# Sliding and forgetting attention: logits from stacked high and low parts, and value products issued together

## The chip, the cores and the metric

The kernel runs as one launch on one core of a Trainium2 chip. The metric is device time in microseconds (us). The median of three runs of the kernel before is 2165.17 us (2159.99 to 2167.82).

## The reference, cut to what matters

The network has two layers. Each mixes 512 tokens of width 1024 by four branches (sliding-window attention, a recurrence called rwkv, forgetting attention, and attention over selected keys), gates and merges them, and runs a feed-forward part: a dense one in the first layer, eight experts in the second. The change touches the two attention branches below, and one step that the third attention branch (`dsa`) shares with them.

```python
def swa_branch(q, k, v, sinks):        # 8 heads, 2 key heads, width 64, window of 128 + chunk of 64
    ...
    logits = jnp.einsum('bcqhgd,bckhd->bchgqk', q, kb).astype(jnp.float32) * ATTN_SCALE
    logits = jnp.where(valid[None, :, None, None, None, :], logits, -jnp.inf)
    m = jnp.maximum(jnp.max(logits, axis=-1, keepdims=True), sink)
    e = jnp.exp(logits - m)
    p = e / (jnp.sum(e, axis=-1, keepdims=True) + jnp.exp(sink - m))
    o = jnp.einsum('bchgqk,bckhd->bcqhgd', p.astype(v.dtype), vb)

def fox_branch(q, k, v, f_logit, f_bias):   # 4 heads of width 64
    log_f = jax.nn.log_sigmoid(f_logit.astype(jnp.float32) + f_bias)
    c = jnp.cumsum(log_f, axis=1).transpose(0, 2, 1)
    for blk in range(S // FOX_BLOCK):       # blocks of 128 queries, keys up to the block's end
        logits = jnp.einsum('bqhd,bkhd->bhqk', q[:, lo:hi], k[:, :hi]).astype(jnp.float32) * ATTN_SCALE
        logits = logits + c[:, :, lo:hi, None] - c[:, :, None, :hi]
        logits = jnp.where(causal, logits, -jnp.inf)
        p = jax.nn.softmax(logits, axis=-1)
        outs.append(jnp.einsum('bhqk,bkhd->bqhd', p.astype(v.dtype), v[:, :hi]))
```

## The kernel before

All of a layer's tokens are kept transposed, split into a high part (`xh`, rounded to the type fp32r) and a low part (`xl`, what is left). A projection (`proj_b`) loads a block of 128 columns of `w_in`, splits it into `whi` (ScalarE, L98) and `wlo` (VectorE, L99) and issues 8 times three matmuls of 512 columns (`mm3`, L111 to L113). Gates, branch outputs and the feed-forward part are made of the same three matmuls.

A mixer runs projections for rwkv, then the rwkv recurrence (a long chain of small matmuls; it inverts 64x64 blocks on VectorE, `invert16`, with stores and loads through memory that GpSimd issues, L737 to L759, and PE takes the result up at L849), the values of all branches (`v_proj`), forgetting attention (`fox`), sliding attention (`swa`), the index of the selected keys (`index`), attention over them (`dsa`), and the merge. The program is written in this order; a scheduler of the framework sets the order of each engine's instructions when the kernel is built, by priority and by when it expects operands. The recurrence has the highest priority, so that PE's row of instructions mixes it with attention and with projections and gates. Engines then run their rows strictly in that order.

In `fox` and `swa`, queries and keys of two heads share a tile of 128 rows, 64 rows to a head, in full fp32 (`qk`, `dup`). The logits of one head and one block of 128 queries are one matmul that contracts 64 rows (L584 in `fox`, L540 in `swa`), with 128 to 512 columns, added in PSUM to a mask (L583, L536) and in `fox` to the sums of the forget gates (L582, with the selector `sel`). `dsa` and `index` already use the other form: `qk_split` puts a head's high part in 64 rows and its low part in the other 64, `dup_split` puts the high part of a key twice above each other and likewise the low part, and `dot` (L425, L426) adds two fp32r matmuls that contract 128 rows. `attend` (L462 to L490) is the softmax: maximum on VectorE, exponential on ScalarE, scaling on VectorE, transposes on PE (L487) and a copy. `quad` runs a block for the four heads of two tiles: with up to 256 keys two heads to a call of `attend`, above that one. Its value products (L512) contract 128 keys and give 64 rows each, the even head in PSUM rows 0 to 63, the odd head in rows 64 to 127. PSUM holds one buffer each of `ps_s` (logits), `ps_t` (transposes) and `ps_o` (outputs).

Of the kernel before, what the change touches and what calls it, by code (L numbers as in the profile page):

```python
# [9 lines left out]
F32 = mybir.dt.float32  # L10
# [8 lines left out]
P = 128  # L19
# [17 lines left out]
TAGS = dict(rw=26, qk=10, o=12, pt=7, v=4, x=8, lc=4)  # L37
# [19 lines left out]
class Net:  # L57
# [292 lines left out]
    def mixer(self, layer):  # L350
# [20 lines left out]
    def qk(self, layer, c0):  # L371

        out = []
        for j in range(2):
            ps = self.proj_b(layer, (c0 + j * P, P))
            t = self.bt("qk")
            with self.tc.high_priority():
                self.nc.scalar.copy(t, ps)
            out.append(t)
        return out  # L380

    def qk_split(self, layer, c0, tag):
# [4 lines left out]
        for j in range(2):  # L387
# [10 lines left out]
    def dup(self, ps):  # L398

        nc = self.nc  # L400
        out = []
        for par, me, ot in HALVES:
            t = self.bt("qk")
            nc.scalar.copy(t[0:64], ps[me])
            nc.vector.tensor_copy(t[64:128], ps[me])
            out.append(t)
        return out

    def dup_split(self, ps):

        nc = self.nc
        out = []
        for par, me, ot in HALVES:
            h, l = self.bt("qk", F32R), self.bt("qk", F32R)
            nc.scalar.copy(h[me], ps[me])
            nc.vector.tensor_sub(l[me], ps[me], h[me].bitcast(F32))
            nc.scalar.copy(h[ot], h[me])
            nc.vector.tensor_copy(l[ot], l[me])
            out.append((h, l))
        return out  # L420

    def dot(self, ps, q, k, b, nk, start):

        q = q[:, b * P:(b + 1) * P]
        self.nc.tensor.matmul(ps, q, k[0][:, :nk], start=start, stop=False)  # L425
        self.nc.tensor.matmul(ps, q, k[1][:, :nk], start=False, stop=True)  # L426
# [65 lines left out]

    def quad(self, b, nk, logits, kblocks, vcol, o, nsink=None):

# [4 lines left out]
        for g0 in range(0, 2, nhu):  # L499
# [28 lines left out]
    def swa(self, layer, kv, q, k):  # L528
# [19 lines left out]
    def fox(self, layer, q, k):  # L548
        nc = self.nc

# [19 lines left out]
        cx, ct = self.bt("pt", F32R), self.bt("pt", F32R)  # L570
# [15 lines left out]
        for g in range(2):  # L586
            self.tap(f"o_fox{g}", o[g][0].bitcast(F32))
# [1266 lines left out]
```

## Time and profile before

| | |
|---|---|
| median of three runs | 2165.17 us |
| the profiled execution's own time | 2165.19 us |
| its span in the trace | 2163.5 us |
| PE busy | 2090.9 us, 97% |
| DVE busy | 1343.8 us, 62% |
| ACT busy | 902.2 us, 42% |
| POOL busy | 151.9 us, 7% |

PE is TensorE's matmuls, PEld its weight loads, DVE VectorE, ACT ScalarE, POOL GpSimd. Matmuls overlap in the trace: an entry's duration runs to its last result, while the next one starts earlier. What a matmul costs the engine is therefore read from start to start. An entry `64*128 64x512` names the rows that are contracted and the columns of the array in use (64*128), and then the rows and columns of the operand that streams. A group in a timeline gives the number of records at its end.

### The profile page before, as it was taken

What the parts mean: (1) busy time and instruction counts of PE and PEld (TensorE: products, weight loads), DVE (VectorE), ACT (ScalarE), POOL (GpSimd) and SP (SyncE); (2) the same over time, 40 slices, a digit from 0 to 9 for tenths busy, and PEclk for the clock granted to TensorE, in tenths of its full rate; (3) what the DMA queues carried; (4) which work ended last, traced back from release to release, by engine and by line L of the source; (5) the groups of instructions that cost most, each with busy time, mean ns of one, the idle gap of its engine ahead of it and who ended that gap; (6) DMA issues with size and microseconds to landing.
All of it is one profiled execution on the core that took longest, in us unless ns stands there. A gap on an engine that the chain in (4) does not pass through costs nothing. (4 is left out here: it accounts for less than half of the span.)

```text
span 2163.5 us, 31132 instructions
## 1 busy us (share of the span) xinstructions
PE 2090.9 (97%) x11252; PEld 1598.0 (74%) x11252; DVE 1343.8 (62%) x2688; ACT 902.2 (42%) x1551; POOL 151.9 (7%) x211
## 2 busy tenths in 40 slices
PE   8999999999999999999999999999998999999994
PEld 7766667778888888888776667778886667677663
DVE  5755678744463333236664678844577877788778
ACT  3444532332332222213444443332326666677663
POOL 1020110000000000000001110000000000000034
PEclk9999999999999999999999999999999999999997
DMA  5220112243343333334221112223258888898872
GB/s 168 76 62 26 46 52 76 78 124 96 97 151 98 98 97 106 116 96 121 75 55 33 46 53 69 69 78 98 92 188 309 298 291 326 302 325 314 291 274 86
DMA packets 275535, 295.07 MB, mean 136 GB/s; under 512 B 23908, under 2 KB 203976, under 8 KB 275368
## 3 DMA queue, kind: packets, MB, share of 16 engines
q1 hardware_dynamic: 268296, 274.42, 39.1%
q0 software_dynamic: 7072, 18.49, 2.7%
q8 instruction: 97, 1.59, 0.3%
q14 instruction: 70, 0.57, 0.1%
HBM read 277.26 MB, written 15.60 MB: 135 GB/s over the span
## 5 line engine op out<-in xcount | busy, mean ns | idle before, releaser
L99 DVE TENSOR_TENSOR wlo<-wraw,whi 128x1024 fp32r<-128x1024 f32 (+1 forms) x218 | 265.7, 1219 | 388.9 <-ACT whi L98 378.5
L113 PE MATMUL ps_mm<-xh,wlo 128*128 128x512 f32 (+1 forms) x1288 | 496.5, 386 | 3.1 <-DVE rs L259 3.1
L98 ACT CAST whi<-wraw 128x1024 fp32r<-128x1024 f32 (+1 forms) x218 | 228.1, 1046 | 650.5 <-PE ps_mm L112 403.1
L111 PE MATMUL ps_mm<-xh,whi 128*128 128x512 f32 (+1 forms) x1288 | 496.4, 386 | 0.8 <-ACT whi L98 0.4
L112 PE MATMUL ps_mm<-xl,whi 128*128 128x512 f32 (+1 forms) x1288 | 494.6, 384 | 0.5 <-DVE xl L233 0.5
L113 PEld LDWEIGHTS ps_mm<-xh,wlo 128*128 128x128 f32 x1288 | 243.3, 189 | 53.1 <-issue 7.7
L111 PEld LDWEIGHTS ps_mm<-xh,whi 128*128 128x128 f32 x1288 | 243.5, 189 | 52.8 <-issue 8.8
L112 PEld LDWEIGHTS ps_mm<-xl,whi 128*128 128x128 f32 x1288 | 243.6, 189 | 48.8 <-issue 5.5
L1153 DVE TENSOR_TENSOR wlo<-mwraw,whi 128x1024 fp32r<-128x1024 f32 (+1 forms) x98 | 124.2, 1281 | 18.0 <-ACT whi L1152 15.6
L1152 ACT CAST whi<-mwraw 128x1024 fp32r<-128x1024 f32 (+1 forms) x98 | 95.9, 1005 | 15.5 <-PE ps_t L1503 9.7
L490 ACT COPY bt_pt<-ps_t 128x512 f32<-128x512 f32 (+2 forms) x80 | 41.8, 522 | 129.5 <-PE ps_t L487 128.8
L462 DVE TENSOR_REDUCE mx<-ps_s 128x2 f32<-128x512 f32 (+3 forms) x80 | 48.7, 609 | 53.5 <-PE ps_s L584 21.4
L1153 DVE TENSOR_TENSOR mwlo<-mwraw,mwhi 128x1024 fp32r<-128x1024 f32 (+1 forms) x62 | 71.9, 1175 | 6.5 <-ACT mwhi L1152 6.0
L471 ACT ACTIVATE bt_pt<-ps_s,mx 128x256 f32<-128x256 f32 (+3 forms) x128 | 62.2, 489 | 18.3 <-DVE mx L465 7.4
L260 POOL TENSOR_TENSOR rs<-rs,mhalf 128x1 f32<-128x1 f32 x16 | 13.8, 860 | 699.0 <-DVE rs L259 699.0
L1152 ACT CAST mwhi<-mwraw 128x1024 fp32r<-128x1024 f32 (+1 forms) x62 | 61.0, 998 | 3.0 <-DMA mwraw<-in_exp_w_dram 1.8
L512 PE MATMUL ps_o<-bt_pt,bt_v 128*64 128x128 f32 (+1 forms) x408 | 60.7, 322 | 0.4 <-ACT bt_pt L490 0.4
L1114 DVE TENSOR_TENSOR bt_pt<-bt_pt,ps_mm 128x512 f32<-128x512 f32 x22 | 15.1, 688 | 70.7 <-PE ps_mm L113 63.3
L612 DVE MAX8 m<-bt_pt 128x8 f32<-128x256 f32 (+2 forms) x96 | 53.5, 558 | 2.1
L1153 DVE TENSOR_TENSOR wlo<-ring,whi 128x1024 fp32r<-128x1024 f32 (+1 forms) x45 | 51.4, 1159 | 2.5 <-ACT whi L1152 1.5
L613 DVE MATCH_REPLACE8 bt_pt<-m,bt_pt 128x256 f32<-128x256 f32 (+2 forms) x96 | 52.1, 543 | 0.0
L112 PE MATMUL ps_mm<-bt_o,whi 128*128 128x512 f32 x128 | 51.5, 402 | 0.0
(716 smaller groups left out, 4133.8 us busy)
## 6 DMA issues: line engine op xcount, KB each, us to landing
mwraw<-in_exp_w_dram SPq DMA_DIRECT2D x124, 512.0 KB, 6.5
wraw<-in_w_in_dram SPq DMA_DIRECT2D x106, 512.0 KB, 3.5
wraw<-in_ffn_w_dram SPq DMA_DIRECT2D x66, 512.0 KB, 3.7
ring<-in_exp_w_dram SPq DMA_DIRECT2D x60, 512.0 KB, 6.4
wraw<-in_exp_w_dram SPq DMA_DIRECT2D x32, 512.0 KB, 7.0
mwraw<-in_exp_w_dram SPq DMA_DIRECT2D x36, 384.0 KB, 5.6
wraw<-in_w_branch_dram SPq DMA_DIRECT2D x20, 512.0 KB, 3.5
wraw<-in_w_out_dram SPq DMA_DIRECT2D x16, 512.0 KB, 3.6
```

Of the source, the lines that this page charges most:

```text
L98: nc.scalar.copy(h, src)
L99: (low or nc.vector).tensor_sub(l, src, h.bitcast(F32))
L111: mm(ps, wh, xh, start=start, stop=False)
L112: mm(ps, wh, xl, start=False, stop=False)
L113: mm(ps, wl, xh, start=False, stop=stop)
L462: nc.vector.tensor_reduce(mx[:, 0:nh], s3, op=OP.max, axis=AX.X)
L471: nc.scalar.activation(p3[:, h], s3[:, h], AF.Exp, bias=nm[:, h:h + 1], scale=0.125, accum_out=mx[:, 4 + h:5 + h])
L512: nc.tensor.matmul(ot[64 * par:64 * par + 64, (g0 + h) * P:(g0 + h + w) * P], self.v[kblocks[kb]][:, c:c + 64], pts[par][:, i * P:(i + w) ...
L612: nc.vector.max(m8, sc[:, :nk])
L613: nc.vector.match_replace(sc[:, :nk], m8, sc[:, :nk], REPL)
L1152: self.chain("hi", lambda: nc.scalar.copy(hi[:, :n], src))
L1153: self.chain("lo", lambda: nc.vector.tensor_sub(lo[:, :n], src, hi[:, :n].bitcast(F32)))
```

## The change

Both attention branches take the form that `dsa` had. `fox` runs once per group of two heads instead of once for four: `forget` makes the forget sums first, and each group then has one tile of queries by `qk_split` and one of keys by `dup_split`. `swa` gets its keys by `dup_split` and its queries by `qk_split`. `dot` gains an offset of the first key. `dup_split` makes the high and the low part of both heads first, at high priority, and the copies to the other 64 rows after. In `quad` and `fox` the value products go through `sums`: it starts with the odd head, whose softmax is made last, alternates the heads, and ties all later products of the block behind the first (`issue_after`), for `dsa` too. Eight kilobytes more per partition are held by tiles of the tag `qk` (14 instead of 10 tiles of 512 fp32), and the scratch in which GpSimd writes its DMA descriptors is set to 8192 bytes per partition (before, the framework's default of 16384).

```diff
-TAGS = dict(rw=26, qk=10, o=12, pt=7, v=4, x=8, lc=4)
+TAGS = dict(rw=26, qk=14, o=12, pt=7, v=4, x=8, lc=4)
...
-        fq, fk = self.qk(layer, FOX0), self.qk(layer, FOX0 + 256)
-        self.fox(layer, fq, fk)
-        sk = self.dup(self.proj_b(layer, (SWA0 + 512, P)))
+        self.forget()
+        for g in range(2):
+            q, = self.qk_split(layer, FOX0 + g * P, "qk", 1)
+            k = self.dup_split(self.proj_b(layer, (FOX0 + 256 + g * P, P)))
+            self.fox(g, q, k)
+        sk = self.dup_split(self.proj_b(layer, (SWA0 + 512, P)))
         for kv in range(2):
-            q = self.qk(layer, SWA0 + 256 * kv)
-            self.swa(layer, kv, q, sk[kv])
+            q = self.qk_split(layer, SWA0 + 256 * kv, "qk")
+            self.swa(kv, q, sk[kv])
         iq = self.qk_split(layer, DSA0 + 384, "qk")
         k, ik = self.dup_split(self.proj_b(layer, (DSA0 + 256, 64), (DSA0 + 640, 64)))
...
-    def qk(self, layer, c0):
-
+    def qk_split(self, layer, c0, tag, n=2):
+
+
+        nc = self.nc
         out = []
-        for j in range(2):
-            ps = self.proj_b(layer, (c0 + j * P, P))
-            t = self.bt("qk")
-            with self.tc.high_priority():
-                self.nc.scalar.copy(t, ps)
-            out.append(t)
-        return out
-
-    def qk_split(self, layer, c0, tag):
-
-
-        nc = self.nc
-        out = []
-        for j in range(2):
+        for j in range(n):
             ps = self.proj_b(layer, (c0 + j * P, P))
             t = [self.bt(tag, F32R) for _ in range(2)]
             with self.tc.high_priority():
...
     def dup_split(self, ps):
 
         nc = self.nc
-        out = []
-        for par, me, ot in HALVES:
-            h, l = self.bt("qk", F32R), self.bt("qk", F32R)
-            nc.scalar.copy(h[me], ps[me])
-            nc.vector.tensor_sub(l[me], ps[me], h[me].bitcast(F32))
+        out = [(self.bt("qk", F32R), self.bt("qk", F32R)) for _ in HALVES]
+        with self.tc.high_priority():
+            for (par, me, ot), (h, l) in zip(HALVES, out):
+                nc.scalar.copy(h[me], ps[me])
+                nc.vector.tensor_sub(l[me], ps[me], h[me].bitcast(F32))
+        for (par, me, ot), (h, l) in zip(HALVES, out):
             nc.scalar.copy(h[ot], h[me])
             nc.vector.tensor_copy(l[ot], l[me])
-            out.append((h, l))
         return out
 
-    def dot(self, ps, q, k, b, nk, start):
-
+    def dot(self, ps, q, k, b, nk, start, k0=0, skip=False):
+
+        mm = self.nc.tensor.matmul
         q = q[:, b * P:(b + 1) * P]
-        self.nc.tensor.matmul(ps, q, k[0][:, :nk], start=start, stop=False)
-        self.nc.tensor.matmul(ps, q, k[1][:, :nk], start=False, stop=True)
+        mm(ps, q, k[0][:, k0:k0 + nk], start=start, stop=skip, skip_group_check=skip)
+        mm(ps, q, k[1][:, k0:k0 + nk], start=False, stop=True, skip_group_check=skip)
...
+    def sums(self, args):
+
+        mm = self.nc.tensor.matmul
+        first = None
+        for ps, v, p, start, stop in args:
+            with ExitStack() as st:
+                if first is not None:
+                    st.enter_context(self.tc.issue_after(first.ins))
+                m = mm(ps, v, p, start=start, stop=stop)
+            first = first or m
+
...
-            w = nhu if vcol(0, 0) == vcol(1, 0) else 1
-            for h in range(0, nhu, w):
-                for kb in range(nkb):
-                    for par in range(2):
-                        c = vcol(g0 + h, par)
-                        i = kb * nhu + h
-                        nc.tensor.matmul(ot[64 * par:64 * par + 64, (g0 + h) * P:(g0 + h + w) * P],
-                                         self.v[kblocks[kb]][:, c:c + 64], pts[par][:, i * P:(i + w) * P],
-                                         start=kb == 0, stop=kb == nkb - 1)
+            self.sums([(ot[64 * par:64 * par + 64, g0 * P:(g0 + nhu) * P], self.v[kblocks[kb]][:, vcol:vcol + 64],
+                        pts[par][:, kb * nhu * P:(kb + 1) * nhu * P], kb == 0, kb == nkb - 1)
+                       for kb in range(nkb) for par in (1, 0)])
...
-                r = slice(64 * par, 64 * par + 64)
                 for g in gs:
-                    nc.tensor.matmul(s3[:, g], q[g][r, b * P:(b + 1) * P], k[r, kbl[0] * P:(b + 1) * P], start=False,
-                                     stop=True, skip_group_check=True)
-
-            self.quad(b, nk, logits, kbl, lambda g, par: VC_SWA + kv * 64, o,
+                    self.dot(s3[:, g], q[g][par], k, b, nk, False, kbl[0] * P, True)
...
+    def forget(self):
+
+        nc = self.nc
         z = self.bp.tile([P, 3, TB, 4], F32, name="fz", tag="fz")
...
-        cx, ct = self.bt("pt", F32R), self.bt("pt", F32R)
-        nc.scalar.activation(cx, cps, AF.Copy, scale=-8.0)
+        self.cx, ct = self.bt("pt", F32R), self.bt("pt", F32R)
+        nc.scalar.activation(self.cx, cps, AF.Copy, scale=-8.0)
...
+    def fox(self, g, q, k):
+
+        nc = self.nc
+        o = self.new_o(("fox", g))
         for b in range(TB):
             nk = P * (b + 1)
-
-            def logits(gs, par, s, s3, b=b, nk=nk):
-                r = slice(64 * par, 64 * par + 64)
-                for i, g in enumerate(gs):
-                    nc.tensor.matmul(s3[:, i], self.sel[:, 2 * g + par:2 * g + par + 1].to_broadcast([P, P]), cx[:, :nk], start=True, stop=False)
+            nh = 2 if nk <= 256 else 1
+            pts = []
+            for p0 in range(0, 2, nh):
+                s = self.ps("s")
+                s3 = s[:, :nh * nk].rearrange("p (h k) -> p h k", h=nh)
+                for i in range(nh):
+                    h = 2 * g + p0 + i
+                    nc.tensor.matmul(s3[:, i], self.sel[:, h:h + 1].to_broadcast([P, P]), self.cx[:, :nk], start=True,
+                                     stop=False)
                     nc.tensor.matmul(s3[:, i, b * P:], self.identb, self.m_causal, start=False, stop=False)
-                    nc.tensor.matmul(s3[:, i], q[g][r, b * P:(b + 1) * P], k[g][r, :nk], start=False, stop=True)
-            self.quad(b, nk, logits, list(range(b + 1)), lambda g, par: VC_FOX + (2 * g + par) * 64, o)
-        for g in range(2):
-            self.tap(f"o_fox{g}", o[g][0].bitcast(F32))
+                    self.dot(s3[:, i], q[p0 + i], k[p0 + i], b, nk, False)
+                pt = self.attend(s3, nh, nk)
+                pts += [[pt[:, (kb * nh + i) * P:(kb * nh + i + 1) * P] for kb in range(b + 1)] for i in range(nh)]
+            ot = self.ps("o")
+            c = VC_FOX + 2 * g * 64
+            self.sums([(ot[64 * par:64 * par + 64, 0:P], self.v[kb][:, c + 64 * par:c + 64 * par + 64], pts[par][kb],
+                        kb == 0, kb == b) for kb in range(b + 1) for par in (1, 0)])
+            self.put_o(o, slice(b * P, (b + 1) * P), ot[:, 0:P])
...
-    nc = bacc.Bacc("TRN2", target_bir_lowering=False, num_devices=1)
+    nc = bacc.Bacc("TRN2", target_bir_lowering=False, num_devices=1, dynamic_dma_scratch_size=8192)
```

The next piece is PE's row in the first layer at the end of `fox`, before. `L584` are logits, `L512` value products, `L849` the recurrence, `L111` to `L113` projections; the number after x counts equal instructions in a row.

```order
L849 MATMUL ps_r<-bt_rw 64x64
L512 MATMUL ps_o<-bt_pt,bt_v 64x128 x7
L582 MATMUL ps_s<-bt_pt,sel 128x512
L583 LDWEIGHTS identb
L583 MATMUL ps_s<-m_causal,identb 128x128
L584 MATMUL ps_s<-bt_qk 128x512
L849 MATMUL ps_r<-bt_rw 64x64 x15
L487 MATMUL ps_t<-ident,bt_pt 128x128 x4
L111 MATMUL ps_mm<-xh,whi 128x512
L112 MATMUL ps_mm<-xl,whi 128x512
L849 MATMUL ps_r<-bt_rw 64x64 x16
L512 MATMUL ps_o<-bt_pt,bt_v 64x128
```

The same engine, changed kernel, at the end of a group of `fox`: `L407` and `L408` are the two matmuls of `dot`, `L483` value products, `L469` transposes.

```order
L575 MATMUL ps_s<-bt_pt,sel 128x128
L577 LDWEIGHTS identb
L577 MATMUL ps_s<-m_causal,identb 128x128
L407 MATMUL ps_s<-bt_qk 128x128
L408 MATMUL ps_s<-bt_qk 128x128
L469 MATMUL ps_t<-ident,bt_pt 128x128 x4
L575 MATMUL ps_s<-bt_pt,sel 128x128
L577 LDWEIGHTS identb
L577 MATMUL ps_s<-m_causal,identb 128x128
L407 MATMUL ps_s<-bt_qk 128x128
L408 MATMUL ps_s<-bt_qk 128x128
L483 MATMUL ps_o<-bt_pt,bt_v 64x128 x8
```

The single matmul over 64 rows has become two over 128 rows. Of a block's eight value products one stood alone (the last row before is the first of the next block) and seven together; now all eight stand together.

Next, PE's row in `swa`, first layer, before: `L540` are logits of two heads, `L512` value products.

```order
L512 MATMUL ps_o<-bt_pt,bt_v 64x256
L113 MATMUL ps_mm<-xh,wlo 128x512
L111 MATMUL ps_mm<-xh,whi 128x512
L536 LDWEIGHTS identb
L536 MATMUL ps_s<-m_swa,identb 128x512
L540 MATMUL ps_s<-bt_qk 128x256 x2
L487 MATMUL ps_t<-ident,bt_pt 128x128 x4
L112 MATMUL ps_mm<-xl,whi 128x512
L113 MATMUL ps_mm<-xh,wlo 128x512
L111 MATMUL ps_mm<-xh,whi 128x512
L112 MATMUL ps_mm<-xl,whi 128x512
L512 MATMUL ps_o<-bt_pt,bt_v 64x256 x3
```

And in the changed kernel, with the recurrence's `L819` near by:

```order
L524 LDWEIGHTS identb
L524 MATMUL ps_s<-m_swa,identb 128x512
L407 MATMUL ps_s<-bt_qk 128x256
L408 MATMUL ps_s<-bt_qk 128x256
L407 MATMUL ps_s<-bt_qk 128x256
L408 MATMUL ps_s<-bt_qk 128x256
L112 MATMUL ps_mm<-xl,whi 128x512
L819 MATMUL ps_r<-bt_rw 128x128 x4
L113 MATMUL ps_mm<-xh,wlo 128x512
L469 MATMUL ps_t<-ident,bt_pt 128x128 x4
```

The two logits of 64 rows after the mask have become four matmuls of `dot`. Over PE's whole row the shape of the array (64 or 128 rows contracted by 32, 64 or 128 columns) changes from one instruction to the next 725 times before and 530 times now, counted over the whole program, branches that are not taken included. The value products of all three branches, 136 of 128 columns and 68 of 256, stand before in 85 unbroken rows: 20 of one, 2 of three, 8 of five and 10 of seven with 128 columns, and 31 of one, 5 of two and 9 of three with 256. Now they stand in 46: 4 of two, 6 of four, 8 of six and 7 of eight, and 2 of one, 5 of two and 14 of four. VectorE has 44 instructions more and ScalarE 28 more; GpSimd and the DMA queue of SyncE have as many as before.

## Rows read from the trace of the kernel before

**Rows 1.** Page, parts 1 and 2: PE busy; granted clock by slice.
```profile
PE 2090.9 (97%) x11252; PEld 1598.0 (74%) x11252; DVE 1343.8 (62%) x2688; ACT 902.2 (42%) x1551; POOL 151.9 (7%) x211
...
PEclk9999999999999999999999999999999999999997
```

**Rows 2.** Windows: us; busy us of PE, PEld, DVE, ACT, POOL; clock, DMA.
```profile
100.00:200.00 100.00, 99.82 (x739) 68.68 (x737) 55.01 (x165) 41.72 (x118) 12.55 (x22) 1.00 0.18 48
200.00:300.00 100.00, 99.31 (x679) 67.24 (x679) 67.70 (x240) 45.32 (x139) 14.61 (x24) 1.00 0.18 48
300.00:415.00 115.00, 112.61 (x638) 86.02 (x635) 97.10 (x241) 37.98 (x77) 2.95 (x2) 0.99 0.26 73
```

**Rows 3.** Waits of PE, 100 to 300 us: total us, times, longest.
```profile
PE ps_r L886 <- ACT xak L880: 0.7, 1, 0.7
```

**Rows 4.** Timeline of PE from 168 us: start us, us, instruction, records.
```profile
168.03 0.40 PE L582 MATMUL ps_s<-bt_pt,sel 128*128 128x512 f32 x1
168.28 0.23 PE L583 MATMUL ps_s<-m_causal,identb 128*128 128x128 bf16 x1
168.44 1.12 PE L584 MATMUL ps_s<-bt_qk 64*128 64x512 f32 x2
169.49 0.50 PE L113 MATMUL ps_mm<-xh,wlo 128*128 128x512 f32 x1
169.82 0.60 PE L487 MATMUL ps_t<-ident,bt_pt 128*128 128x128 f32 x4
...
170.49 0.40 PE L112 MATMUL ps_mm<-xl,whi 128*128 128x512 f32 x1
170.73 0.40 PE L113 MATMUL ps_mm<-xh,wlo 128*128 128x512 f32 x1
171.06 0.33 PE L849 MATMUL ps_r<-bt_rw 64*64 64x64 f32 x2
171.31 1.09 PE L512 MATMUL ps_o<-bt_pt,bt_v 128*64 128x128 f32 x14
172.33 0.50 PE L582 MATMUL ps_s<-bt_pt,sel 128*128 128x512 f32 x1
```

**Rows 5.** Timeline of PE at 252 us: one pair of sliding-window logits.
```profile
252.05 1.13 PE L540 MATMUL ps_s<-bt_qk 64*128 64x256 f32 x4
253.10 0.50 PE L111 MATMUL ps_mm<-xh,whi 128*128 128x512 f32 x1
```

**Rows 6.** Timeline of PE at 288 us: one dot of the index, then projection.
```profile
288.42 0.28 PE L425 MATMUL ps_s<-bt_qk 128*128 128x256 f32 x1
288.53 0.28 PE L426 MATMUL ps_s<-bt_qk 128*128 128x256 f32 x1
288.66 0.40 PE L113 MATMUL ps_mm<-xh,wlo 128*128 128x512 f32 x1
```

**Rows 7.** Timeline of PE at 130 us: one value product of 128 columns alone.
```profile
130.49 0.43 PE L512 MATMUL ps_o<-bt_pt,bt_v 128*64 128x128 f32 x2
130.85 0.50 PE L112 MATMUL ps_mm<-xl,whi 128*128 128x512 f32 x1
```

**Rows 8.** Timeline of PE at 184 us: one value product of 256 columns alone.
```profile
183.90 0.65 PE L512 MATMUL ps_o<-bt_pt,bt_v 128*64 128x256 f32 x2
184.48 0.33 PE L876 MATMUL ps_r<-bt_rw 64*64 64x64 f32 x4
```

**Rows 9.** Groups by line, DVE, 100 to 300 us: busy us, mean ns.
```profile
L394 DVE TENSOR_TENSOR bt_qk<-ps_mm,bt_qk 64x512 fp32r<-64x512 f32 x4 | 2.8, 689 | 0.1
...
L418 DVE CAST bt_qk<-bt_qk 64x512 fp32r<-64x512 f32 x2 | 0.8, 422 | 0.1
```

**Rows 10.** Groups by line, ACT, 100 to 300 us.
```profile
L392 ACT CAST bt_qk<-ps_mm 64x512 fp32r<-64x512 f32 x4 | 2.3, 583 | 0.0
```

**Rows 11.** Timeline of POOL from 152 us: start us, us, records.
```profile
152.52 3.98 POOL L756 DMA_DIRECT2D inv<-bt_rw  x7 [19.45 <-DVE bt_pt L481]
```

**Rows 12.** Line L759, its DMAs: issue to landing.
```profile
DMA to landing us min/median/max: 2.7/2.9/3.5
```

More of the change, by code (lines that the diff above doesn't have):

```diff
@@ L396, in qk_split @@
         return out
-    def dup(self, ps):
-        nc = self.nc
-        out = []
-        for par, me, ot in HALVES:
[L403 to L407, printed above, removed]
     def dup_split(self, ps):
         nc = self.nc
-        out = []
-        for par, me, ot in HALVES:
-            h, l = self.bt("qk", F32R), self.bt("qk", F32R)
-            nc.scalar.copy(h[me], ps[me])
-            nc.vector.tensor_sub(l[me], ps[me], h[me].bitcast(F32))
+        out = [(self.bt("qk", F32R), self.bt("qk", F32R)) for _ in HALVES]
[4 more added lines that the diff above has]
+        for (par, me, ot), (h, l) in zip(HALVES, out):
             nc.scalar.copy(h[ot], h[me])
             nc.vector.tensor_copy(l[ot], l[me])
-            out.append((h, l))
         return out
-    def dot(self, ps, q, k, b, nk, start):
+    def dot(self, ps, q, k, b, nk, start, k0=0, skip=False):
+        mm = self.nc.tensor.matmul
         q = q[:, b * P:(b + 1) * P]
-        self.nc.tensor.matmul(ps, q, k[0][:, :nk], start=start, stop=False)
-        self.nc.tensor.matmul(ps, q, k[1][:, :nk], start=False, stop=True)
+        mm(ps, q, k[0][:, k0:k0 + nk], start=start, stop=skip, skip_group_check=skip)
+        mm(ps, q, k[1][:, k0:k0 + nk], start=False, stop=True, skip_group_check=skip)
     def v_proj(self, layer):
@@ L526, in put_o, with swa @@
         self.nc.vector.tensor_sub(lo[:, ts], ps, hi[:, ts].bitcast(F32))
-    def swa(self, layer, kv, q, k):
+    def swa(self, kv, q, k):
         nc = self.nc
@@ L537, in logits @@
                                  self.m_swa[:, None, 256 - nk:].to_broadcast([P, 2, nk]), start=True, stop=True)
-                r = slice(64 * par, 64 * par + 64)
                 for g in gs:
-                    nc.tensor.matmul(s3[:, g], q[g][r, b * P:(b + 1) * P], k[r, kbl[0] * P:(b + 1) * P], start=False,
-                                     stop=True, skip_group_check=True)
-            self.quad(b, nk, logits, kbl, lambda g, par: VC_SWA + kv * 64, o,
+                    self.dot(s3[:, g], q[g][par], k, b, nk, False, kbl[0] * P, True)
+            self.quad(b, nk, logits, kbl, VC_SWA + kv * 64, o,
                       lambda g0, par, n: self.nsink[:, 4 * kv + par:4 * kv + 4:2])
@@ L546, in swa @@
             self.tap(f"o_swa{2 * kv + g}", o[g][0].bitcast(F32))
-    def fox(self, layer, q, k):
+    def forget(self):
         nc = self.nc
@@ L569, in fox @@
                                  stop=True, skip_group_check=True)
-        cx, ct = self.bt("pt", F32R), self.bt("pt", F32R)
-        nc.scalar.activation(cx, cps, AF.Copy, scale=-8.0)
+        self.cx, ct = self.bt("pt", F32R), self.bt("pt", F32R)
+        nc.scalar.activation(self.cx, cps, AF.Copy, scale=-8.0)
         nc.scalar.activation(ct[32:64], cps[32:64], AF.Copy, scale=-8.0)
-        nc.vector.scalar_tensor_tensor(cx[32:64], cps[32:64], -8.0, ct[32:64].bitcast(F32), op0=OP.mult,
+        nc.vector.scalar_tensor_tensor(self.cx[32:64], cps[32:64], -8.0, ct[32:64].bitcast(F32), op0=OP.mult,
@@ L574, in fox @@
                                        op1=OP.subtract)
-        o = [self.new_o(("fox", g)) for g in range(2)]
+    def fox(self, g, q, k):
+        nc = self.nc
+        o = self.new_o(("fox", g))
         for b in range(TB):
             nk = P * (b + 1)
-            def logits(gs, par, s, s3, b=b, nk=nk):
-                r = slice(64 * par, 64 * par + 64)
-                for i, g in enumerate(gs):
-                    nc.tensor.matmul(s3[:, i], self.sel[:, 2 * g + par:2 * g + par + 1].to_broadcast([P, P]), cx[:, :nk], start=True, stop=False)
-                    nc.tensor.matmul(s3[:, i, b * P:], self.identb, self.m_causal, start=False, stop=False)
-                    nc.tensor.matmul(s3[:, i], q[g][r, b * P:(b + 1) * P], k[g][r, :nk], start=False, stop=True)
-            self.quad(b, nk, logits, list(range(b + 1)), lambda g, par: VC_FOX + (2 * g + par) * 64, o)
@@ L589, in index @@
+            ot = self.ps("o")
[3 more added lines that the diff above has]
+            self.put_o(o, slice(b * P, (b + 1) * P), ot[:, 0:P])
+        self.tap(f"o_fox{g}", o[0].bitcast(F32))
     def index(self, q, k):
@@ L628, in logits @@
                     self.dot(s3[:, i], q[g][par], k, b, nk, False)
-            self.quad(b, nk, logits, list(range(b + 1)), lambda g, par: VC_DSA, o)
+            self.quad(b, nk, logits, list(range(b + 1)), VC_DSA, o)
         for g in range(2):
```

## Prediction

> **What bounds the kernel now.** I read the page first, then windows, waits and the timeline of PE. The page shows PE busy for 97% of the span, with the clock at full speed in nearly every slice [rows 1]. That number alone says little, since matmuls overlap in the trace. So I took the stretches where the two changed branches run, 100 to 300 us in the first layer (the second layer runs the same code once more). PE is busy there for 99.8 and 99.3 of each 100 us at a granted clock of 1.00, its full 2.4 GHz, and in all 200 us its waits come to a single one of 0.7 us [rows 2, 3]. VectorE is busy for 55 and 68 us of 100 and ScalarE for 42 and 45. PE is the bound, and everything else fits beside it. What the change takes from PE's row there should shorten the program by as much, as long as PE does not begin to wait. Start to start in the timeline tells what an instruction costs PE.
>
> **Prices on PE.** Four readings give nearly all of them.
>
> The first is a change of shape. Between projections of 512 columns PE steps by 0.24 us (L112 at 170.49 to L113 at 170.73). The L113 just before the 64x64 matmuls of L849 takes 0.33, and the L113 that follows the 64-row L584 takes 0.33 as well (169.49 to 169.82) [rows 4]. So a change of shape costs about 0.09 us on the last matmul of the old shape and as much or a little more on the first of the new, 0.18 to 0.20 us in all. I take 0.19.
>
> The second is a logit of 64 rows. One with 512 columns leaves two records and occupies PE from 168.44 to 169.49, 1.05 us [rows 4]. Less an entry and an exit (0.09 to 0.10 each) its own time is 0.85 to 0.87; I take 0.85. Two with 256 columns occupy 1.05 us together [rows 5], so 0.85 for two and 0.43 for one: per column the same. With 384 columns that makes 0.64, with 128 columns 0.21.
>
> The third is the new form. In the index the first matmul of a dot with 256 columns takes 0.11 and the second 0.13 us [rows 6], 0.24 for the pair. With 512 columns a full-shape fp32r matmul takes 0.23 to 0.25 (L582 from 168.03 to 168.28) [rows 4], so a pair 0.46 to 0.50; I take 0.46, as the projections step. Between them 384 columns make 0.35 a pair. No row here shows a pair of 128 columns. It lies between half of the pair of 256 and the whole of it, 0.12 and 0.24; I take 0.22, close to the row.
>
> The fourth is the value products. One of 128 columns alone takes 0.36 us [rows 7], seven in one row take 1.02 (171.31 to 172.33) [rows 4]. Products of the odd and the even head use different columns of the array. If two neighbours run side by side, seven in the order odd, even, odd and so on are four steps, and 0.36 = a + s, 1.02 = a + 4s give a step s of 0.22 us and 0.14 for changing shape. One of 256 columns alone takes 0.58 [rows 8], so a step of 0.43. The first product standing alone therefore wastes half of its step, and the seven waste half of their last.
>
> **The sum.** Counts are of both layers.
>
> (a) The logits themselves. Removed: 24 of 128 columns, 56 of 256, 8 of 384 and 8 of 512 (`fox` has 8 of each size, `swa` 16 of 128 and 48 of 256). Each becomes a pair. 56 x (0.43 - 0.24) = 10.6; 8 x (0.64 - 0.35) = 2.3; 8 x (0.85 - 0.46) = 3.1; 128 columns 24 x (0.21 - 0.22), nothing (between 2 less and 1 more by the bounds). Together 16 us less.
>
> (b) The pairing of value products. By the rows of the order, 128 columns take 20 x 1 + 2 x 2 + 8 x 3 + 10 x 4 = 88 steps before and 4 x 1 + 6 x 2 + 8 x 3 + 7 x 4 = 68 now; 256 columns 31 + 5 + 9 x 2 = 54 before and 2 + 5 + 14 x 2 = 35 now. 20 x 0.22 + 19 x 0.43 = 12.6 us less.
>
> (c) The changes of shape, 195 fewer: 195 x 0.19 = 37 us less (35 to 39 by its bounds). Most stand around L584 and L540, the rest around value products.
>
> That is 66 us less on PE. Projections, masks, forget sums and transposes stay as many as they were.
>
> (d) New work elsewhere. VectorE gets 44 instructions, per layer 16 subtractions of 0.69 and 6 copies of 0.42 [rows 9], 27 us in both layers. ScalarE gets 28 of about 0.58 [rows 10], 16 us. They lie beside PE's projections. In 100 to 300 us VectorE is busy for 123 us; with 14 more, and about 34 us less of PE's time around them, its share goes from 61% to some 83%; ScalarE's from 44% to some 57%. So VectorE has less room, but it still is not the bound. What is queued behind the new instructions on VectorE are the low parts of weights (L99) and the softmax steps, and PE waits for both. Bounds for PE's new waits: none, or all of VectorE's extra 27 us. What speaks for the low end is that 0.7 us of wait in 200 [rows 3] leave the program some slack at each hand-over; I take 5 us. From 300 to 415 us, where the selection of keys keeps VectorE busy for 97 of 115 us [rows 2], neither kind of logits stands in PE's row, so nothing changes but the value products of `dsa`.
>
> (e) The inversion in rwkv has a latency of its own. PE would wait at L849 if the attention placed before it ran out sooner. The scheduler mixes in more projections there, and I count it in the 5 us.
>
> (f) The smaller scratch for DMA descriptors. The row of GpSimd shows seven stores issued in 3.98 us, 0.57 each, without a wait between them [rows 11], while such a DMA takes 2.9 us to land [rows 12]: about five are under way at once. I take 0; the other end is the rival below. Could it gain? More room for descriptors would not come from a smaller scratch, so below nothing is excluded.
>
> Sum: -66 + 5 = -61. The profiled execution took 2165.2 us (span 2163.5), within 0.1 us of the median, so the prediction is 2104 us. With no new waits it is 2099; were the dot's 512 columns 0.50 instead of 0.46 it would be 0.6 us more.
>
> **Rivals.** *VectorE takes back what it can.* All 27 us of added VectorE work turn up as PE's waits. For it: the high-priority splits stand ahead of softmax steps, and PSUM has one buffer for logits, so a late maximum or exponential stops the next logits. Against it: VectorE idles for 77 us of the 200. 2165 - 66 + 27 = 2126.
>
> *A dot whose second weight load does not hide.* Both matmuls of a dot load the same queries into the same rows. In the index the second follows the first by 0.11 us [rows 6], with nothing exposed; where a first matmul comes after another shape, 0.10 is. If all 192 matmuls of the new dots paid it, 19 us would be given back: 2165 - 66 + 19 + 5 = 2123. The Trainium skill, "TensorE: Matmul & The Clock Gate", section "Part 3: Packing small matmuls", says that weight loads overlap running matmuls only when the row group differs. By that rule this rival would be the result; the 0.11 us row disagrees, so its chance is small.
>
> *Changes of shape are free.* If the 0.19 us per change were time that PE would lose anyway (to the same operands being late), (c) falls out: 2165 - 29 + 5 = 2141. Against it: the 0.33 us recur in front of and behind every other shape, whoever made the operands. That the change doesn't do what it says, by the scheduler pulling dots and products apart, is ruled out for the products by the order; hi and lo of a dot are parted here and there, which costs nothing while both neighbours have the full shape.
>
> *The slower side: the inversion's DMAs queue up.* With half the scratch, each of the 8 stores and 4 loads after an inversion (L756, L759) could wait until the one before has landed: 12 x (2.9 - 0.57) = 28 us per inversion, 112 for the four, and PE stands at L849 once its projections there are used up: 2165 - 66 + 112 = 2211. It decides from 17 us per inversion on, which is 7 of 12 DMAs waiting. Against it: the seven stores went out back to back, so the scratch was not full with five under way; whether half of it holds as many, no row shows.
>
> **How the numbers follow.** The forecast gets 0.78, its own range 2095 to 2114 (no new waits and 0.20 per change, to 15 us of waits). VectorE's rival gets 0.10, the unhidden load 0.03, the free changes 0.03, the DMAs 0.06. Left out of 8 in 10 may be the free changes, the DMAs and some of the forecast's edges; the range is 2089 to 2129. A measurement of this kernel tells 0.5%, 11 us, from no change. Faster by more than that holds in all cases but the last and a few of the middle ones: faster 0.92, same 0.02, slower 0.06.
>
> **What would show it.** In the profile after: pairs of dot matmuls at 0.24 (256 columns) and 0.46 us (512) start to start, with neighbours at 0.24 rather than 0.33; rows of 8 value products of 128 columns in 1.02 us and of 4 of 256 in about 1.0; PE's waits in the two stretches still a few us, with VectorE near 80% there. The first layer's attention and everything behind it should begin some 31 us earlier, the rest of the program unchanged. The prediction is wrong if PE's waits on `bt_pt`, `wlo` or `bt_qk` come to more than some 15 us, if PE stands at L848 (L849 before) after the inversions, or if the second matmul of a dot steps at over 0.2 us with 256 columns.

## The result

The changed kernel takes 2131.47 us (median of four runs, 2129.68 to 2134.61); the kernel before took 2165.99 beside it. The ratio is 0.9847 [0.9824, 0.987], 34.5 us faster. Forecast were 61 us, 2104; the time lies 2.5 us above the range. The profiled execution took 2129.7 us (span 2127.9).

First the page after, PE's busy time and granted clock by slice, which answers [rows 1]:

```profile
PE 2040.7 (96%) x11252; PEld 1590.5 (75%) x11252; DVE 1365.3 (64%) x2732; ACT 918.8 (43%) x1579; POOL 150.3 (7%) x211
...
PEclk9999999999999999999999999999999999999997
```

The windows, with the columns of [rows 2], and PE's waits from 100 to 300 us, which answer [rows 3]:

```profile
100.00:200.00 100.00, 98.46 (x795) 74.46 (x793) 69.22 (x193) 49.88 (x129) 12.56 (x22) 1.00 0.24 58
200.00:300.00 100.00, 94.46 (x766) 69.36 (x766) 69.85 (x237) 51.41 (x156) 14.66 (x24) 0.98 0.19 48
```

```profile
PE ps_mm L111 <- ACT gate L977: 1.8, 1, 1.8
PE ps_r L885 <- ACT xak L879: 1.6, 3, 0.9
PE ps_t L469 <- DVE bt_pt L463: 1.0, 3, 0.4
...
```

PE idles for 7.1 us of these 200 instead of 0.9, mostly for the recurrence (its rows write `ps_r`) and a gate, and the clock is a little lower in the second hundred. VectorE is busy for 70 us of 100, not for the 83 that I had forecast.

The new instructions themselves, in PE's timeline (start us, us, instruction, records): a pair of sliding-window logits, which answers [rows 5], a logit of forgetting attention over 512 keys, which answers the start of [rows 4], and eight value products:

```profile
254.19 0.39 PE L524 MATMUL ps_s<-m_swa,identb 128*128 128x512 bf16 x1
254.23 0.47 PE L407 MATMUL ps_s<-bt_qk 128*128 128x256 f32 x1
254.54 0.27 PE L408 MATMUL ps_s<-bt_qk 128*128 128x256 f32 x1
254.65 0.28 PE L407 MATMUL ps_s<-bt_qk 128*128 128x256 f32 x1
254.77 0.28 PE L408 MATMUL ps_s<-bt_qk 128*128 128x256 f32 x1
254.88 0.40 PE L112 MATMUL ps_mm<-xl,whi 128*128 128x512 f32 x1
...
146.04 0.40 PE L575 MATMUL ps_s<-bt_pt,sel 128*128 128x512 f32 x1
146.28 0.23 PE L577 MATMUL ps_s<-m_causal,identb 128*128 128x128 bf16 x1
146.32 0.48 PE L407 MATMUL ps_s<-bt_qk 128*128 128x512 f32 x1
146.64 0.39 PE L408 MATMUL ps_s<-bt_qk 128*128 128x512 f32 x1
146.86 0.39 PE L113 MATMUL ps_mm<-xh,wlo 128*128 128x512 f32 x1
...
153.21 1.09 PE L483 MATMUL ps_o<-bt_pt,bt_v 128*64 128x128 f32 x16 [0.31 <-ACT bt_pt L472]
154.23 0.50 PE L112 MATMUL ps_mm<-xl,whi 128*128 128x512 f32 x1
```

Mask and two dots take 0.69 us (254.19 to 254.88); by my prices, with the mask's 512 columns at 0.23, it is 0.23 + 2 x 0.24 = 0.71. The matmul behind them steps 0.23 (254.88 to 255.12). Eight value products take 1.02 (153.21 to 154.23), as forecast. The logit over 512 keys takes 0.82 from 146.04 to 146.86; with 0.07 for the short mask (0.16 in [rows 4], less an entry of 0.09) it would be 0.25 + 0.07 + 0.46 = 0.78. So where a group can be seen by itself, it costs what it should, but for a few hundredths. Only the sum of such neighbours is a price: the mask of 512 columns steps by 0.04 and the dot behind it by 0.31, together what 512 and 256 columns take elsewhere.

The loss is elsewhere. In a state step of the recurrence PE makes one product (L875), ScalarE copies it, and PE goes on with the copy (L885, L886); there are 16 such steps. This is PE in the second layer, at the last four of them:

```profile
1249.76 1.15 PE L848 MATMUL ps_r<-bt_rw 64*64 64x64 f32 x32
1251.87 0.45 PE L875 MATMUL ps_r<-bt_rw 64*64 64x64 f32 x8 [0.96 <-DVE bt_rw L866]
1252.69 0.34 PE L885 MATMUL ps_r<-xak,bt_rw 64*64 64x64 f32 x4 [0.37 <-ACT xak L879]
...
1253.88 0.45 PE L875 MATMUL ps_r<-bt_rw 64*64 64x64 f32 x8 [0.46 <-ACT bt_rw L891]
1254.69 0.34 PE L885 MATMUL ps_r<-xak,bt_rw 64*64 64x64 f32 x4 [0.36 <-ACT xak L879]
...
1259.31 0.49 PE L885 MATMUL ps_r<-xak,bt_rw 64*64 64x64 f32 x4 [0.92 <-ACT xak L879]
...
```

From the end of L848 to 1261.7 us, for 11 us, PE does nothing but the recurrence's state steps (2 us each, the last 3), and waits in each, mostly for copies on ScalarE. In the kernel before two or three matmuls of projections stood in each of these gaps:

```profile
1283.27 0.45 PE L876 MATMUL ps_r<-bt_rw 64*64 64x64 f32 x8 [0.36 <-DVE bt_rw L867]
1283.68 0.50 PE L111 MATMUL ps_mm<-xh,whi 128*128 128x512 f32 x1
1284.03 0.39 PE L112 MATMUL ps_mm<-xl,whi 128*128 128x512 f32 x1
1284.35 0.34 PE L886 MATMUL ps_r<-xak,bt_rw 64*64 64x64 f32 x4
```

By the order of PE's row, 6 of the 16 state steps have nothing between L875 and L885 (1 of 16 before).

The table is the trace of PE summed from start to next start, waits included, by what each matmul is for, in us, over both layers (E5 is the run `e5_dsaq` below; the last row is the span less PE's busy time on the page):

| | before | after | E5 |
|---|---|---|---|
| logits, masks, forget sums of `fox` and `swa` | 75.4 | 50.0 | 49.9 |
| value products of attention | 54.3 | 36.3 | 36.5 |
| recurrence | 114.5 | 126.6 | 113.9 |
| transposes of `attend` | 27.8 | 24.4 | 25.2 |
| projections, gates, merges | 995.4 | 992.2 | 992.7 |
| span | 2163.5 | 2127.9 | 2110.8 |
| PE idle, by the page | 72.6 | 87.2 | 75.2 |

The recurrence, in which nothing was edited, costs 12 us more. The experiments ask whether that, a wrong price of shape changes, or dearer dots is the reason.

### The profile page after: what moved, and what is told of

Same layout as the page of the kernel before. It is cut to its first block, busy times and chain, and to the rows that moved or that the text cites. A ratio compares the mean times of both kernels' runs of the same rounds, so it can differ in the third digit from the quotient of the medians.

```text
span 2127.9 us, 31168 instructions
## 1 busy us (share of the span) xinstructions
PE 2040.7 (96%) x11252; PEld 1590.5 (75%) x11252; DVE 1365.3 (64%) x2732; ACT 918.8 (43%) x1579; POOL 150.3 (7%) x211
## 5 line engine op out<-in xcount | busy, mean ns | idle before, releaser
L111 PE MATMUL ps_mm<-xh,whi 128*128 128x512 f32 (+1 forms) x1288 | 494.3, 384 | 3.2 <-ACT gate L977 2.6
L113 PE MATMUL ps_mm<-xh,wlo 128*128 128x512 f32 (+1 forms) x1288 | 494.3, 384 | 3.1 <-DVE rs L259 3.1
L111 PEld LDWEIGHTS ps_mm<-xh,whi 128*128 128x128 f32 x1288 | 243.9, 190 | 49.3 <-ACT gate L977 3.1
L113 PEld LDWEIGHTS ps_mm<-xh,wlo 128*128 128x128 f32 x1288 | 244.0, 190 | 47.4 <-DVE wlo L99 3.4
L453 ACT ACTIVATE bt_pt<-ps_s,mx 128x256 f32<-128x256 f32 (+3 forms) x128 | 62.0, 488 | 16.8 <-DVE mx L447 14.2
L469 PE MATMUL ps_t<-ident,bt_pt 128*128 128x128 f32 x272 | 50.8, 282 | 4.2 <-DVE bt_pt L463 3.2
L111 PE MATMUL ps_mm<-bt_o,whi 128*128 128x512 f32 x128 | 51.2, 400 | 0.4 <-ACT gate L977 0.4
```

The lines of the kernel that those rows point to most:

```text
L111: mm(ps, wh, xh, start=start, stop=False)
L113: mm(ps, wl, xh, start=False, stop=stop)
L453: nc.scalar.activation(p3[:, h], s3[:, h], AF.Exp, bias=nm[:, h:h + 1], scale=0.125, accum_out=mx[:, 4 + h:5 + h])
L469: nc.tensor.transpose(pt[:, i * P:(i + 1) * P], p3[:, h, kb * P:(kb + 1) * P], self.ident)
```

## The experiments

In the expectations theory W is "the prices held, and PE waits for the recurrence", S "a change of shape is cheap", D "the dots are dear".

**E1 and E2: one half each.** E1 is the kernel before with its value products through `sums`; E2 is the changed kernel with the old loops:

```diff
-            self.sums([(ot[...], self.v[kblocks[kb]][...], pts[par][...], kb == 0, kb == nkb - 1) ...])
+            for kb in range(nkb):
+                for par in range(2):
+                    nc.tensor.matmul(ot[...], self.v[kblocks[kb]][...], pts[par][...], start=kb == 0, stop=kb == nkb - 1)
```

> The kernel before with only its value products issued together (odd head first, later ones tied behind the first); logits of 64 rows stay. In PE's row 43 fewer unbroken rows of value products and 54 fewer changes of shape than before (725 to 671). Theory W (the prices were right, and what is missing of the forecast is PE waiting, above all for the recurrence when the attention beside it has run out): 12.6 us of pairing and 54 x 0.19 = 10 us of shape changes, 23 less, some of it given back in waits: 2142 to 2150. Theory S (a change of shape costs only (34 - 23.6) / 195 = 0.05 us, the rest as forecast): 12.6 + 3 = 15 less, 2150. Theory D (the new dots are dearer than forecast, the products' part is right): 2142.

> The changed kernel with the value products as before (even head first, each issued when the scheduler likes); logits from stacked high and low parts. 133 fewer changes of shape than before (725 to 592). Theory W: 16 us of the logits' own time and 133 x 0.19 = 25, 41 less, less some 10 to 15 of waits: 2135 to 2139. Theory S: 16 + 7 - 5 = 18 less, 2147. Theory D: little is left of the logits' own 16 us: 25 - 5 = 20 less, 2145. Under W the two parts together gain less than the sum of each alone, since the later the recurrence is, the less stands beside it.

E1 took 2146.34 us, 0.9906 [0.9892, 0.992], 21 less than before: near the 23 of W and D, not the 15 of S. E2 took 2154.00, 0.9939 [0.9926, 0.9952], 13 less: below what any theory said. The halves add up (34.3 of 34.5), against what I said under W. So nearly all that is missing is in the logits' half. In E2's row 8 of 16 state steps have nothing beside them, and in its profiled execution, which with 2163.3 us was 9 longer than the median, the recurrence takes 134.5 us, 20 more than before; the logits cost 48.3, less than those of the changed kernel. E1 has one empty step, and its recurrence takes 116.2.

**E3 and E4: the price of a change of shape.** A matmul of zeros stands between the two matmuls of each new dot, over 64 rows (E3) or 128 (E4):

```diff
+        mm(ps[:, 0:4], self.identb[0:64, :], self.zer[0:64, 0:4], start=False, stop=False, skip_group_check=True)
```

> The changed kernel with one tiny matmul of zeros (4 columns, bf16) between the two matmuls of each of the 96 dots of sliding and forgetting attention. It contracts 64 rows, so it brings 192 of 195 changes of shape back (722 against 530). To be read against the same matmul over 128 rows in the next run. Theory W: 188 x 0.19 = 36 us over the next run, less what PE's waits of the changed kernel absorb, at least 25. Theory S: 188 x 0.05 = 10 us over the next run.

> The same as the run before, but the tiny matmul contracts all 128 rows: no change of shape (534 against 530). It costs a step of 0.04 us or so and a load of the identity and of the queries: 96 x 0.05 to 96 x 0.2, 5 to 19 us over the changed kernel (2136 to 2150), the same by all theories. If theory D holds because weight loads behind a short matmul are not hidden, it is the high end: each of these 96 matmuls adds one such load, 96 x 0.19 = 18.

E3 took 2154.06, E4 2139.61 (ratios 0.9945 [0.9932, 0.9957] and 0.9873 [0.9858, 0.9887]): E4 is 8 us over the changed kernel, as expected. Between them lie 14.5 us for 188 changes, 0.08 each, where W said 25 to 36 and S 10. PE's timeline shows why, E3 first, then E4:

```profile
197.51 0.47 PE L409 MATMUL ps_s<-bt_qk 128*128 128x256 f32 x1
197.91 0.17 PE L411 MATMUL ps_s<-zer,identb 64*128 64x4 bf16 x1
198.02 0.38 PE L412 MATMUL ps_s<-bt_qk 128*128 128x256 f32 x1
198.24 0.28 PE L409 MATMUL ps_s<-bt_qk 128*128 128x256 f32 x1
```

```profile
263.97 0.47 PE L409 MATMUL ps_s<-bt_qk 128*128 128x256 f32 x1
264.28 0.18 PE L411 MATMUL ps_s<-zer,identb 128*128 128x4 bf16 x1
264.31 0.36 PE L412 MATMUL ps_s<-bt_qk 128*128 128x256 f32 x1
264.51 0.28 PE L409 MATMUL ps_s<-bt_qk 128*128 128x256 f32 x1
```

The dot's first matmul steps by 0.40 instead of 0.31 and the tiny one by 0.11 instead of 0.03, but the matmul behind it has lost 0.08 already in E4 (264.31 to 264.51, 0.20 instead of 0.12), and loses hardly more in E3 (198.02 to 198.24, 0.22). As I read it, behind so short a matmul PE waits for weights anyway (a load takes 0.19 us), and part of the second shape change hides in that wait. So the price is real (0.09 on the matmul in front), but it isn't always paid in full. Theory W's number for this test was wrong, and the test doesn't say what a change costs between long matmuls.

**E5: room for the work beside the recurrence.** Tiles of one tag share a fixed number of buffers, and a new one waits until an old one is given up. The edit takes the queries of `dsa` from the recurrence's tag to another:

```diff
-        self.dsa(self.qk_split(layer, DSA0, "rw"), k, masks)
+        self.dsa(self.qk_split(layer, DSA0, "qk"), k, masks)
```

> The changed kernel, but the queries of attention over selected keys are kept in tiles of the tag qk (14 of them) instead of rw, which the recurrence holds till its end. In PE's row two to four projections then stand again between all 16 of the recurrence's state steps (L875, L885); in the changed kernel six gaps in a row's end had none. 551 changes of shape against 530. Theory W (missing: PE waits for the recurrence, since the work that could stand beside it is blocked behind tiles that the recurrence holds): the stalls of 8 us at 1250 to 1261 us and 3 at 290 to 294 go and the clock dips behind them (5 us), less 21 x 0.09 to 0.19 for changes of shape: 9 to 14 us faster than the changed kernel, 2117 to 2123. Theories S and D (the prices of shape changes or dots were wrong): no gain beyond 3 us, 2128 to 2135.

E5 took 2114.57 us, 0.9764 [0.9749, 0.9779]: 17 less than the changed kernel (the kernel before took 2166.0 and 2166.4 beside the two), more than W asked for, and the fastest of the kernels that compute everything. The same place in its timeline:

```profile
1244.88 0.45 PE L875 MATMUL ps_r<-bt_rw 64*64 64x64 f32 x8
1245.26 0.45 PE L407 MATMUL ps_s<-bt_qk 128*128 128x384 f32 x1
1245.54 0.34 PE L408 MATMUL ps_s<-bt_qk 128*128 128x384 f32 x1
1245.73 0.39 PE L113 MATMUL ps_mm<-xh,wlo 128*128 128x512 f32 x1
1246.04 0.34 PE L885 MATMUL ps_r<-xak,bt_rw 64*64 64x64 f32 x4
...
1247.60 0.45 PE L875 MATMUL ps_r<-bt_rw 64*64 64x64 f32 x8
```

And windows at that place, the changed kernel first, E5 second:

```profile
1245.00:1262.00 17.00, 11.71 (x191) 8.94 (x187) 15.28 (x42) 6.29 (x14) 0.00 (x0) 0.90 0.13 32
1262.00:1275.00 13.00, 13.00 (x95) 9.64 (x91) 7.28 (x28) 3.42 (x10) 0.76 (x1) 0.86 0.01 1
```

```profile
1245.00:1262.00 17.00, 17.00 (x178) 11.97 (x178) 13.91 (x43) 5.21 (x14) 0.00 (x0) 1.00 0.10 32
1262.00:1275.00 13.00, 12.91 (x79) 9.79 (x77) 10.25 (x43) 3.53 (x8) 1.04 (x1) 1.00 0.06 14
```

PE's 5.3 us of idling are gone, and so is the dip of the granted clock behind them. The work was there all along, but it had no place to go. In the changed kernel the two projections for the queries of `dsa` are done by 1213.3 and 1222.5 us, and their results sit in two of the three `ps_mm` buffers until tiles of `rw` come free: the copies (L384) run at 1257.8 us and after, at the end of the state steps. In E5 they run at 1219 to 1227 us, and projections behind them go on. The first of these copies, the changed kernel first:

```profile
1257.78 1.18 ACT L384 CAST bt_rw<-ps_mm 64x512 fp32r<-64x512 f32 x2
```

```profile
1219.40 1.19 ACT L384 CAST bt_qk<-ps_mm 64x512 fp32r<-64x512 f32 x2 [0.69 <-PE ps_s L408]
```

Not all 17 us lie beside the recurrence. From the second layer's last output projection (L1036) to the end, where neither edit reaches, the traces show 553.4 us in the changed kernel and 550.1 in E5 (551.8 before, L1037), so some 14 us are the mixers'.

**E6 and E7: both kernels without the recurrence** (`self.rwkv(layer, pr)` left out).

> The kernel before without the recurrence (its output is replaced by a copy of two of its projections), so that nothing of PE's row waits for it. Only a base for the next run. The recurrence's matmuls take some 57 us a layer in the trace, and 239 changes of shape go with it: 2167 - 114 - what its neighbours lost to changes, about 2030 to 2050.

> The changed kernel without the recurrence. Against the run before it has 224 fewer changes of shape (486 to 262) and the same new logits and products. Theory W: the whole of what PE's row should give, 16 + 12 + 224 x 0.19 = 70 us less than the run before, at least 60. Theory S (a change of shape costs 0.05): 16 + 12 + 11 = 39 less. Theory D: some 50 less. Should VectorE have taken the time back, it still does so here: 45 or less.

They took 2031.38 and 1993.67 us (0.9389 and 0.9204 of the kernel before): 37.7 apart, not 60 to 70. This speaks against W as I had put it, and for D, S or VectorE. PE's longest waits from 60 us to the end of the first layer's attention, in E7 (in E6 the largest entry is 1.1 us):

```profile
PE ps_t L470 <- DVE bt_pt L464: 6.4, 6, 3.4
```

Without the recurrence PE waits for the softmax instead, where projections beside it have run out; PE's steps in the first layer's attention that are over 0.45 us longer than their columns come to some 12 us in E7 and 2.5 in E6. With a lower mean clock (0.982 against 0.989) this may make up most of what is missing. That is argued from sums and not tested, and the two profiled executions (2026.3 and 1997.1 us) are only 29 us apart. The pair doesn't settle the prices.

**E8: half of VectorE's added work taken away.** The second matmul of a new dot reads the high part of the keys again; the low parts are not made.

> The changed kernel without the low parts of keys in sliding and forgetting attention: the second matmul of a dot reads the high part again, so PE's work is the same, while VectorE loses 6 subtractions of 0.69 and 6 copies of 0.42 us a layer, 13 us of the 27 that the change gave it. If VectorE's added work turned into PE's waits one for one, 13 us faster than the changed kernel (2118). Theory W and the others: within 4 us of it, 2127 to 2135.

2126.01 us, 0.9816 [0.9801, 0.9831]: 5.5 us less than the changed kernel, a little more than I allowed, for 13 us of VectorE's time by the prices and 9 by the pages (1365.3 to 1356.2). Four of it are the recurrence's (122.5 us instead of 126.6). The order of PE's row differs too, with 4 empty state steps instead of 6, so the run can't tell VectorE's work from that. Either way VectorE's work is not the bulk.

**E9 to E11: shorter logits without dots, shapes or VectorE work.** E9 is E5's edit on the kernel before. E10 takes the kernel before and halves the time of its 64-row logits by rounding both operands to fp32r (tiles of `qk` and `dup` made as `F32R`); E11 is E10 with E5's edit.

> The kernel before, with the queries of attention over selected keys in tiles of the tag qk instead of rw: the edit that made the changed kernel 17 us faster. Before, the recurrence's 16 state steps had projections between them in all but one gap, and PE waited 0.7 us for it. Theory W (the recurrence became the limit only because the attention beside it was made shorter): nothing to gain here, within 4 us of the kernel before, 2163 to 2170. If the edit is an independent gain (tiles of rw late for the merge in any case): some 10 to 17 us faster, 2150 to 2157.

> The kernel before, but its 96 logits of 64 rows take operands rounded to fp32r and so one pass of the array instead of two; the low parts are left out. Changes of shape (733 against 725), value products, VectorE's work and the order of the branches stay. By the rows of before a pass over 64 rows costs about half of 0.85, 0.43, 0.21: 8 x 0.43 + 8 x 0.32 + 56 x 0.21 + 24 x 0.1 = 20 us less for PE. In its row three of the recurrence's sixteen state steps have nothing beside them, and three more one matmul. Theory W: a part of the 20 us comes back as PE waiting for the recurrence and as clock, though no dot, no shape and no VectorE work was changed: 5 to 14 us faster, 2152 to 2161. If shortening attention by itself costs nothing: 20 us faster, 2146.

> The run before with the queries of attention over selected keys in tiles of the tag qk: projections stand between nearly all state steps again (one step of sixteen without), and 12 changes of shape more. Theory W: what was lost comes back, less 12 x 0.19 = 2 us: 15 to 18 us faster than the kernel before, 2148 to 2151. If shortening attention by itself costs nothing, no gain over the run before.

E9 took 2165.77, 1.0001 [0.9992, 1.001]; E10 2162.15, 0.9987 [0.9978, 0.9995]; E11 2149.42, 0.9933 [0.992, 0.9946]. E10 gained 3 us, less than the 5 to 14 of W. A pair of sliding-window logits fell to 0.43 us in E10, from 1.05 [rows 5]; PE's steps for logits and masks fell by 28 us, and the recurrence's grew by 23 (137.4). Windows around the end of the recurrence in either layer, before and then E10:

```profile
270.00:330.00 60.00, 59.27 (x509) 41.32 (x508) 45.25 (x133) 23.70 (x60) 7.09 (x11) 1.00 0.18 47
1245.00:1300.00 55.00, 54.64 (x472) 36.66 (x471) 42.35 (x129) 22.93 (x60) 7.17 (x12) 1.00 0.21 58
```

```profile
270.00:330.00 60.00, 52.47 (x448) 37.74 (x447) 43.83 (x130) 17.45 (x42) 8.21 (x13) 0.83 0.15 38
1245.00:1300.00 55.00, 45.74 (x375) 31.90 (x374) 39.93 (x134) 17.83 (x47) 7.17 (x12) 0.84 0.18 48
```

With the queries of `dsa` in other tiles most of it comes back (E11 is 13 us under E10 and 16 under the kernel before; recurrence 116.8), while the same edit is worth nothing on the kernel before. That settles it: the loss needs neither dots nor VectorE nor shapes. Taking logit time away empties the gaps of the recurrence, and what could fill them is blocked behind tiles that the recurrence holds.

Empty state steps (of 16) and the recurrence's PE time, in us, for all runs that have it: E9 0 and 113.4, E5 0 and 113.9, before 1 and 114.5, E1 1 and 116.2, E11 2 and 116.8, E8 4 and 122.5, after 6 and 126.6, E3 7 and 127.9, E4 7 and 128.0, E2 8 and 134.5. E10, with 3 empty and two more with a single matmul, has 137.4: it lost most of its time at another place of the same chain. Of the 12.3 us that PE waited behind the recurrence's matmuls in E10, 8.7 follow L849, where the inversion is taken up:

```profile
297.25 1.15 PE L849 MATMUL ps_r<-bt_rw 64*64 64x64 f32 x32 [1.23 <-DVE bt_rw L867]
299.68 1.97 PE L849 MATMUL ps_r<-bt_rw 64*64 64x64 f32 x32 [1.28 <-DVE bt_rw L862]
```

In the changed kernel it is 2.1 of 8.6 us behind L848, and 6.4 in the state steps.

## Why the prediction was wrong

*(d) and (e), "I take 5 us": the failed step.* I wrote that PE would wait for the recurrence if attention ran out sooner, that "The scheduler mixes in more projections there", and counted that in the 5 us. The scheduler could not: the projections that were left had no place for their results. PE's idle time grew by 14.6 us (72.6 to 87.2), the clock fell behind it, and E5, whose one edit makes room for those projections, runs 17 us faster, 14 of them in the mixers. I had also named one place, L849 (L848 after), where the inversion is taken up; in the changed kernel most waits stand at the state steps behind it. What I could have read: PE's row shows one empty state step of 16 and PE hardly waits [rows 3], so the slack was a few projections, and I took a good part of the 66 us out beside it. The merge of the first layer, which I had 31 us earlier, begins 21 us earlier (its first L111 on `bt_rw` at 509.6 instead of 530.7 us).

*The price of dots in (a): a size, wrong by some 7 us at most.* The 96 new dots with their masks come to 43.4 us, 2.6 of them waits; the dots were priced at 25.2, and the masks make some 8 at the step of their columns. Of the 7 us above that, 2 stand next to another shape, which (c) counts, and 2 behind a transpose, where some of it only moves from one record to the next. "Which costs nothing while both neighbours have the full shape" was wrong for hi and lo parted (29 of the 152 dots of all branches). Here a transpose stands between them:

```profile
272.35 0.30 PE L469 MATMUL ps_t<-ident,bt_pt 128*128 128x128 f32 x1
272.40 0.36 PE L408 MATMUL ps_s<-bt_qk 128*128 128x256 f32 x1
272.60 0.39 PE L113 MATMUL ps_mm<-xh,wlo 128*128 128x512 f32 x1
```

The matmul behind the transpose steps by 0.20 instead of 0.12; the load of the queries takes 0.195 us (mean of the weight loads of L407, 100 to 300 us). But the transpose itself steps by 0.05, where transposes in a row step by 0.11, so that the two lose 0.03 together. Behind the short causal mask a dot over 512 keys loses some 0.06 with its mask (146.28 to 146.64, 0.36, instead of 0.07 + 0.23). The rival of the unhidden load was thus right in a small part, behind short matmuls; the second matmul of a dot, for which it was meant, steps by 0.12 (254.77 to 254.88). The Trainium skill, "TensorE: Matmul & The Clock Gate", section "Part 3: Packing small matmuls", lets a load overlap running matmuls only where the row group differs; the 0.12 against a load of 0.195 into the same rows speaks against it. The Trainium skill, on the same page, section "Back-to-back issue gap", says that load and matmul together set the spacing; the 0.20 behind the matmul of 4 columns in E4 agrees.

*What held.* The value products: E1 gives 21 of the 23 us that (b) and its changes of shape come to. The shape price of 0.19 for the logits: a pair of sliding-window logits with its mask took 1.37 us before (251.73 to 253.10, its end in [rows 5]) and 0.09 on the next matmul; it takes 0.69 now, 0.77 less against 0.76 forecast. The order of the row has the 195 fewer changes, but E3 shows that the price isn't a constant, so the total of (c) is not shown. (f): GpSimd is busy as before (150.3 us against 151.9), and PE waits 2.1 us behind L848, where that rival needed 17 per inversion. VectorE's busy time rose by 21.5 us, not 27, and its share went to 70%, not 83%; by proportion from E8 its work costs some 13 us at most, part of it the same waits that E5 removes. The sums of that rival (2126) and of the unhidden load (2123) lie nearer to 2131 than the forecast, but neither mechanism is what the runs show. A slip without weight: 0.50 instead of 0.46 for the eight dots of 512 columns would be 0.3 us, not 0.6.

*The account.* 61 forecast, 34.5 measured; of the 26.5 missing E5 returns 17, and the dots take at most 7. What is left, 2 or 3 us, or 5 to 6 if only the mixers' part of E5 is counted, the runs can't tell; a shape price below 0.19 in places would be one way.

## What to carry to other kernels

When work is taken from a bound engine that also hosts a serial chain, count the gaps of that chain and ask what will stand in them; an engine without waits in the profile says only that there is enough today. Then look at what holds the next work back: here it was not its own operands but tiles of a shared tag, and a change of one tag was worth half as much as the whole rewrite. And read a matmul's price together with its neighbours: a short step in front of it can stand for time that its own step then shows.

## What was not expected of the hardware

An idle PE costs twice: in E10 PE idled for 16.8 us in the two windows above (1.1 before), and the granted clock stood at 0.83 and 0.84 there (a mean of the two levels, 2.4 and 1.2 GHz) against 1.00 before; in E5, without the idling, it stays at 1.00. It takes no single long wait: in the changed kernel the clock stands at 0.90 from 1245 to 1262 us, where from 1249.8 us on PE runs only the recurrence's small matmuls, with waits of at most 0.96 us between them. The page's clock row by slices of 53 us rounds this away: in the changed kernel it shows 9 throughout the mixers.
